# First-norm operands of a streaming encoder layer: conditioning products between the transposes, group 0 first, group 1 in place

## The chip, the cores and the metric

One Trainium2 chip, one of its cores. The metric is the device time of one execution in microseconds, taken as the median of several runs; the smaller the better. TensorE (PE) multiplies matrices, VectorE (DVE) and ScalarE (ACT) do elementwise work, GpSimd (POOL) too, and SyncE (SP) issues the DMA transfers. Each engine executes its own queue in order; semaphores hold one for another.

## The reference

One inference step of a hybrid encoder layer, for a prompt of 1024 tokens and a sample of 32 (1056 together), model width 1024. All arithmetic is float32:

```python
mod = (silu(c) @ w_ada + b_ada)               # shift1, scale1, gate1, shift2, scale2, gate2
h = rms_norm(x, norm1_g) * (1 + scale1) + shift1
proj = h @ w_in                               # 8192 columns: q, k, v, xin, gb, gc, ga, gb_br
...                                           # differential attention, short convolution, gates, output
x = x + gate1 * (m @ w_out)
h2 = rms_norm(x, norm2_g) * (1 + scale2) + shift2
x = x + gate2 * ((silu(g) * up) @ w_down)     # g, up = split(h2 @ w_gate_up)
```

The change concerns the first two lines only: how h comes to the form in which the first projections use it.

## The kernel before, in words

**Layout.** h is kept transposed in `xnT`: 128 partitions (a channel of one of 8 channel tiles) by 1056 tokens. The tokens are cut into four quarters of 264 columns (`QW`); quarters 0 and 2 are token group 0, quarters 1 and 3 are group 1.

**The multiplications.** `strassen` (from L164) multiplies a 256-column block of weights with one token group by a seven-product scheme in the order of `SEQ`: products on the operands B11, T2, T1, B21, T3, B22, T4, each of twelve matmuls (four channel tiles, three parts, because each float32 factor is split into a rounded high part and a remainder). B11, B12 are the two quarters of the group in channel tiles 0 to 3, B21, B22 those in tiles 4 to 7; T1 = B12 - B11, T2 = B22 - T1, T3 = B22 - B12, T4 = B21 - T2. The results are gathered in PSUM banks X, Y, Z, V: VectorE adds u2 = Y + p1 after product 2 (L188) and w = Z + u2 after product 3 (L191). Product 6 adds into Z again and product 7 into V, so product 6 waits until L191 has read Z and product 7 until L197 has read V.

**The operands.** `split` (L83 to L85) writes an operand: ScalarE casts the high part, VectorE subtracts it to get the remainder. `h_operands(j, g)` (from L389) does this for one channel tile pair j, j + 4 and one group g: four subtractions on VectorE (L398, L399, L403, L406) into small tiles `ht`, and seven splits, all of 264 columns. It is called eight times.

**The order around it.** Conditioning products come first: `ada_load` fetches a 1024 x 128 block of w_ada (seven buffers, shared with the weights), `ada_matmul` (L333) multiplies it, ScalarE copies the row (L335), `ada_close` transposes four rows (L342) and adds the bias (L344, `mod`). x is loaded in nine token tiles (L294), squared on ScalarE (L301), scaled on VectorE (L304), transposed on TensorE (L313) and copied to `xnT` (L315 on ScalarE, L317 on VectorE). `modulate(n)` takes its gain from L377 and applies gain and shift to the prompt's tokens on ScalarE (L384) and to the sample's on VectorE (L386), in place. The loop over j = 0 to 3 does four conditioning products, modulates tiles j and j + 4, and builds the operands of group 0 for j and of group 1 for j - 1; at j = 2 the first weights are split in between (`wstrassen`, L147 to L157, its last remainder on GpSimd). Then h is stored to DRAM (L445), the last group 1 operands follow, and `attention_constants` loads five small rows (L264) and takes an Exp (L271). The first projection `conv_in` runs group 0 and then group 1 with the same weights.

TensorE's queue is in the order of the program. On the other engines a scheduler orders the instructions when the program is built, by its own costs, so the place of an instruction in a queue is not that of its line.

Of the kernel before, what the change touches and what calls it, by code (L numbers as in the profile page):

```python
# [7 lines left out]
F32 = mybir.dt.float32  # L8
# [6 lines left out]
P = 128  # L15
D = 1024
KT = 8
S = 1024
DS = 32
T = S + DS  # L20
# [9 lines left out]
QW = T // 4  # L30
# [4 lines left out]
def f(ap):  # L35
    return ap.bitcast(F32)


def hybrid_layer(tc, x_prompt, x_sample, cache_k, cache_v, state_conv, c_prompt, c_sample,
# [76 lines left out]
    def u_tile():  # L116
        return PSB.tile([P, 512], F32, tag="u", name="u", bufs=6)

    def x_tile():
        return PSB.tile([P, 512], F32, tag="x", name="x", bufs=2)  # L120
# [7 lines left out]
    Top, home = {}, {}  # L128

    def op_slot(i, shape, dtype, name):  # L130
        return (OpA if i < NA else OpB).tile(shape, dtype, tag=f"op{i}", name=name)
# [4 lines left out]
    def wstrassen(srcs):  # L136

        raw = [kt_stage(src) for src in srcs]
        A11, A12, A21, A22 = raw[0][:, :4], raw[0][:, 4:], raw[1][:, :4], raw[1][:, 4:]
        w = {}  # L140

        def parts(o, src, eng=None):
            w[o] = ws_tile()
            split(src, w[o][:, 0], w[o][:, 1], eng)

        parts("A11", A11)
        dve.tensor_sub(A11, A11, A21)  # L147
        S3 = A11
        dve.tensor_add(A21, A21, A22)
        S1 = A21  # L150
        parts("A22", A22)
        dve.tensor_sub(A22, A22, S3)
        S2 = A22
        parts("S2", S2)
        parts("S1", S1)
        parts("A12", A12)
        dve.tensor_sub(A12, A12, S2)  # L157
        S4 = A12
        parts("S3", S3)
        parts("S4", S4, pool)  # L160
        return w
# [72 lines left out]
    E = sb("E", side="right")  # L234
    X0 = sb("X0")
# [6 lines left out]
    def load_rows():  # L242
        for r0, ap in ((R_B, b_ada), (R_G1, norm1_g), (R_G2, norm2_g), (R_CW, conv_w[0]), (R_ST, state_conv[0, 0])):
            row_load(rows[r0:r0 + ap.shape[0] * ap.shape[1] // P, :], ap)
        for u in range(2):
            sp.dma_start(rows[R_GQ:R_GQ + 1, u * HD:(u + 1) * HD], q_norm_g)
        sp.dma_start(rows[R_GS:R_GS + 1, :], sub_norm_g)

    def rows_to_vec():
        pv = x_tile()  # L250
        pe.transpose(pv[:, :P], rows, ident)
        dve.tensor_copy(vec, pv[:, :P])
# [24 lines left out]
    xnT = X0.tile([P, KT, T], F32, name="xnT")  # L277
# [3 lines left out]
    def token_tile(i):  # L281
        return (xp_v[i * P:(i + 1) * P, :], P) if i < 8 else (xs_v, DS)
# [3 lines left out]
    def x_half(i):  # L286
        if i // 2 not in xslots:
            xslots[i // 2] = op_slot(NA + i // 2, [P, 2, T], F32, "xt")
        return xslots[i // 2][:, i % 2, :D]

    def x_load(i):
        src, n = token_tile(i)
        xt = x_half(i)
        sp.dma_start(xt[:n], src)  # L294
        xts[i] = xt, n

    def x_norm(i):

        xt, n = xts[i]
        junk = x_half(9 + i % 2)  # L300
        act.activation(junk[:n], xt[:n], AF.Square, scale=1.0 / 32.0, accum_out=msx[:n, i:i + 1])  # L301
        pool.tensor_scalar(out=rsx[:n, i:i + 1], in0=msx[:n, i:i + 1], scalar1=EPS, scalar2=None, op0=ALU.add)
        pool.tensor_tensor(out=rsx[:n, i:i + 1], in0=rsx[:n, i:i + 1], in1=mhalf[:n, 0:1], op=ALU.pow)
        dve.tensor_scalar(out=xt[:n], in0=xt[:n], scalar1=rsx[:n, i:i + 1], scalar2=None, op0=ALU.mult)  # L304

    def x_transpose(tiles, kts):
        q0 = tiles[0] * P
        w = sum(xts[i][1] for i in tiles)
        for kt in kts:
            pt = u_tile()  # L310
            for j, i in enumerate(tiles):
                xt, n = xts[i]
                pe.transpose(pt[:, j * P:j * P + n], xt[:n, kt * P:(kt + 1) * P], ident[:n, :n])  # L313
            if kt % 2:
                act.copy(xnT[:, kt, q0:q0 + w], pt[:, :w])  # L315
            else:
                dve.tensor_copy(xnT[:, kt, q0:q0 + w], pt[:, :w])  # L317
# [3 lines left out]
    def ada_load(c):  # L321
        v = w_slot([P, KT, P], F32, "adw")
        sp.dma_start(v, wada_v[:, :, c * P:(c + 1) * P])
        ada_v.append((c, v))
# [3 lines left out]
    def ada_matmul():  # L328

        c, v = ada_v.pop(0)  # L330
        pa = x_tile()
        for kt in range(KT):
            pe.matmul(pa[0:2, :P], sc[:, kt:kt + 9:8], v[:, kt, :], start=kt == 0, stop=kt == KT - 1)  # L333
        row = E.tile([2, P], F32, tag=("w", "t")[len(ada_open) % 2], name="adarow", bufs=2)
        act.copy(row, pa[0:2, :P])  # L335
        ada_open.append((c, row))

    def ada_close():
        pb = x_tile()
        done, ada_open[:] = ada_open[:], []  # L340
        for i, (c, row) in enumerate(done):
            pe.transpose(pb[:, 2 * i:2 * i + 2], row, ident[0:2, 0:2])  # L342
        for i, (c, row) in enumerate(done):
            dve.tensor_scalar(out=mod[:, c, :], in0=pb[:, 2 * i:2 * i + 2], scalar1=vec[:, R_B + c:R_B + c + 1],  # L344
                              scalar2=None, op0=ALU.add)
# [30 lines left out]
    def scale_gain(dst, sec, n, row):  # L376
        dve.tensor_scalar(out=dst[:, n, :], in0=mod[:, sec * KT + n, :], scalar1=1.0,  # L377
                          scalar2=vec[:, row + n:row + n + 1], op0=ALU.add, op1=ALU.mult)

    def modulate(n):  # L380

        scale_gain(a1, 1, n, R_G1)
        y = xnT[:, n, 0:S]
        act.activation(y, y, AF.Identity, scale=a1[:, n, 0:1], bias=mod[:, n, 0:1])  # L384
        y = xnT[:, n, S:T]
        dve.tensor_scalar(out=y, in0=y, scalar1=a1[:, n, 1:2], scalar2=mod[:, n, 1:2], op0=ALU.mult, op1=ALU.add)  # L386

    def h_operands(j, g):

        def parts(o, src):  # L390
            t = Top[o, g]
            split(src, t[:, 0, j, :], t[:, 1, j, :])

        b11, b12 = (xnT[:, j, q * QW:(q + 1) * QW] for q in (g, g + 2))
        b21, b22 = (xnT[:, j + 4, q * QW:(q + 1) * QW] for q in (g, g + 2))
        t1, t2, t3 = (X0.tile([P, QW], F32, tag=f"t{i}", name="ht", bufs=1) for i in (1, 2, 1))
        parts("B11", b11)
        dve.tensor_sub(t1, b12, b11)  # L398
        dve.tensor_sub(t2, b22, t1)  # L399
        parts("T2", t2)  # L400
        parts("T1", t1)
        parts("B21", b21)
        dve.tensor_sub(t3, b22, b12)  # L403
        parts("T3", t3)
        parts("B22", b22)
        dve.tensor_sub(t2, b21, t2)  # L406
        parts("T4", t2)

    ada_order = [sec * KT + n for j in range(4) for n in (j, j + 4) for sec in (0, 1)]
    for c in ada_order[:4]:  # L410
        ada_load(c)
    load_rows()
    for i in range(9):
        x_load(i)
    for c in ada_order[4:7]:
        ada_load(c)
    for c in ada_order[7:11]:
        ada_matmul()
        ada_load(c)
    rows_to_vec()  # L420
    ada_close()
    for i in range(9):
        x_norm(i)
        if i % 4 == 3:
            x_transpose(range(i - 3, i + 1), range(KT))
    x_transpose((8,), range(KT))
    for i, (o, g) in enumerate((o, g) for o in OPS for g in (0, 1)):
        home[o, g] = (OpA if i < NA else OpB, f"op{i}")
        Top[o, g] = op_slot(i, [P, 2, 4, QW], F32R, f"{o}{g}")
    for j in range(4):  # L430
        if j:
            for i in range(4):
                ada_matmul()
                if 7 + 4 * j + i < len(ada_order):
                    ada_load(ada_order[7 + 4 * j + i])
            ada_close()
        if j == 2:
            w0 = wstrassen(win_pair(3, 0))
        modulate(j)
        modulate(j + 4)  # L440
        h_operands(j, 0)
        if j:
            h_operands(j - 1, 1)
    for n in range(KT):
        sp.dma_start(h_d[n], xnT[:, n, :])  # L445
    h_operands(3, 1)
    attention_constants()


# [93 lines left out]
    for sec, dst in ((6, ga_d), (7, gb_d)):  # L543
        for p in range(0, KT, 2):
            w = wstrassen(win_pair(sec, p))
            sg = pair_tile()
# [571 lines left out]
    for n in range(KT):  # L1118
        w = wpiece(wao_v[:, :, n * P:(n + 1) * P])
        sg = B.tile([P, T], F32, tag="sg", name="sg", bufs=2)  # L1120
# [5 lines left out]
        for g0, gw in GROUPS:  # L1126
            pt = u_tile()
            unit(pt, w, ot, g0, gw)
            c = slice(g0, g0 + gw)
# [203 lines left out]
    E = sb("E")  # L1333
# [92 lines left out]
    late = [slot(("T4", 0)), xk[:, 0], xk[:, 1]]  # L1426
# [102 lines left out]
```

## Time and profile before

| | us |
|---|---|
| median of 3 runs (2134.64 to 2137.19) | 2136.35 |
| the profiled execution: its own time | 2132.99 |
| its span, from first to last instruction | 2131.2 |
| TensorE busy / VectorE busy / ScalarE busy | 2031.0 / 1351.4 / 847.1 |
| mean granted TensorE clock, of full speed | 0.982 |

The profile page gives busy times per engine and the span in 40 slices; views of the trace give the stages, the instructions in order of time, and what each engine waited for. Times in the trace start at the span's first instruction. A bracket such as [0.93 <-DVE sg L197] says that the engine was idle for 0.93 us in front of the row and that L197 on VectorE ended it. Instructions overlap on an engine's pipeline, so the time from one start to the next can be shorter than the duration shown.

### The profile page before, as it was taken

The page shows a single profiled execution, that of the slowest core. Times are in us where ns is not written, and L with a number is a line of the kernel's source. Part 1 is how long each engine was busy: PE and PEld are TensorE (multiplying, and loading weights), DVE is VectorE, ACT ScalarE, POOL GpSimd, SP SyncE. Part 2 cuts the span into 40 slices and gives each one's busy share as a digit, 9 for nine tenths or more (in the row PEclk, how much of TensorE's full clock was granted, in tenths as well). Part 3 has the DMA queues.
Part 4 walks back from the last instruction along what each step waited for, and adds up shares of the span by engine and source line. Part 5 has one row for each costly group of instructions (what it writes and reads, how often), then busy time and mean ns, then how long its engine had stood idle before and what let it go on. Part 6 is the DMA issues. An engine that isn't in the chain of part 4 may idle for free. (4 is left out here: it accounts for less than half of the span.)

```text
span 2131.2 us, 37806 instructions
## 1 busy us (share of the span) xinstructions
PE 2031.0 (95%) x14339; PEld 1976.7 (93%) x14339; DVE 1351.4 (63%) x3096; ACT 847.1 (40%) x2044; POOL 364.7 (17%) x660
## 2 busy tenths in 40 slices
PE   7799999899999999999899989889999999999999
PEld 5799999899999999999899989879999999989998
DVE  4988799967766776677357974685555555432322
ACT  5522233366666666666222213463332332321210
POOL 1023100033333333333000000012112112100000
PEclk8899999999999999999999999999999999999999
DMA  8422254532211221121388625123222222552321
GB/s 251 151 84 90 71 161 135 192 89 60 68 57 56 62 59 54 50 69 48 114 258 250 198 90 170 53 68 122 71 73 89 70 80 79 172 157 65 99 69 57
DMA packets 298960, 224.42 MB, mean 105 GB/s; under 512 B 15617, under 2 KB 281498, under 8 KB 298778
## 3 DMA queue, kind: packets, MB, share of 16 engines
q1 hardware_dynamic: 298778, 222.00, 34.0%
q8 instruction: 113, 1.85, 0.4%
q14 instruction: 69, 0.57, 0.1%
HBM read 162.46 MB, written 59.49 MB: 104 GB/s over the span
## 5 line engine op out<-in xcount | busy, mean ns | idle before, releaser
L84 ACT CAST ws<-st 128x512 fp32r<-128x512 f32 x360 | 217.2, 615 | 564.4 <-PE u L181 172.9
L181 PE MATMUL u<-op,ws 128*128 128x264 f32 x3168 | 397.3, 285 | 7.8 <-ACT op L84 6.5
L181 PEld LDWEIGHTS u<-op,ws 128*128 128x128 f32 x3168 | 392.4, 189 | 8.4 <-ACT op L84 6.7
L85 DVE TENSOR_TENSOR ws<-st,ws 128x512 fp32r<-128x512 f32 (+1 forms) x322 | 222.6, 699 | 195.3 <-ACT ws L84 192.9
L181 PE MATMUL u<-T,ws 128*128 128x264 f32 x1536 | 198.5, 287 | 1.2 <-DVE sg L197 1.2
L181 PEld LDWEIGHTS u<-T,ws 128*128 128x128 f32 x1536 | 193.5, 190 | 1.8 <-DVE sg L197 1.8
L731 PE MATMUL b<-qw,hA 128*128 128x384 f32 x512 | 186.8, 365 | 2.5 <-DVE adred L366 1.2
L732 PE MATMUL b<-qw,hA 128*128 128x384 f32 x512 | 174.2, 340 | 0.6 <-DVE qw L688 0.6
L733 PE MATMUL b<-qw,hA 128*128 128x384 f32 x512 | 173.8, 339 | 0.0
L1431 PE MATMUL u<-ka,ws 128*128 128x352 f32 x480 | 156.8, 327 | 4.6 <-ACT ka L84 2.8
L1432 PE MATMUL u<-ka,ws 128*128 128x352 f32 x480 | 155.6, 324 | 2.3 <-DVE ka L85 2.3
L181 PE MATMUL u<-B,ws 128*128 128x264 f32 x1152 | 152.1, 287 | 4.6 <-ACT B L84 4.6
L1433 PE MATMUL u<-ka,ws 128*128 128x352 f32 x480 | 155.7, 324 | 0.0
L181 PEld LDWEIGHTS u<-B,ws 128*128 128x128 f32 x1152 | 145.6, 190 | 5.3 <-ACT B L84 4.9
L357 DVE SCALAR_TENSOR_TENSOR adacc<-adw,sc,adacc 128x128 f32<-128x128 f32 x448 | 132.8, 350 | 0.6
L879 ACT ACTIVATE p<-S,nmx,rs 128x128 f32<-128x128 f32 (+5 forms) x144 | 113.1, 787 | 50.1 <-DVE nmx L959 17.0
L85 POOL TENSOR_TENSOR ws<-st,ws 128x512 fp32r<-128x512 f32 x38 | 49.8, 1311 | 445.3 <-ACT ws L84 426.1
L731 PEld LDWEIGHTS b<-qw,hA 128*128 128x128 f32 x512 | 97.7, 191 | 6.4 <-issue 2.1
L732 PEld LDWEIGHTS b<-qw,hA 128*128 128x128 f32 x512 | 97.9, 191 | 1.2 <-DVE qw L688 0.9
L733 PEld LDWEIGHTS b<-qw,hA 128*128 128x128 f32 x512 | 97.2, 190 | 0.0
L1431 PEld LDWEIGHTS u<-ka,ws 128*128 128x128 f32 x480 | 90.6, 189 | 5.6 <-ACT ka L84 3.5
L1432 PEld LDWEIGHTS u<-ka,ws 128*128 128x128 f32 x480 | 90.7, 189 | 3.1 <-DVE ka L85 3.1
(277 smaller groups left out, 4379.8 us busy)
## 6 DMA issues: line engine op xcount, KB each, us to landing
adw<-in_w_ada_dram SPq DMA_DIRECT2D x48, 512.0 KB, 4.0
st<-in_w_gate_up_dram SPq DMA_DIRECT2D x44, 512.0 KB, 4.0
st<-in_w_in_dram SPq DMA_DIRECT2D x43, 512.0 KB, 4.3
sa<-a_d SPq DMA_DIRECT2D x22, 528.0 KB, 3.6
a_d<-xa SPq DMA_DIRECT2D x84, 132.0 KB, 1.7
st<-in_w_in_dram SPq DMA_DIRECT2D x42, 256.0 KB, 2.9
st<-in_w_down_dram SPq DMA_DIRECT2D x16, 512.0 KB, 5.0
h_d<-xnT SPq DMA_DIRECT2D x8, 528.0 KB, 4.3
```

Of the source, the lines that this page charges most:

```text
L84: act.copy(hi, src)
L85: (lo_eng or dve).tensor_sub(lo, src, f(hi))
L181: pe.matmul(q[dst], l, t[:, r, j, :], start=first and j == n == 0, stop=j == 3 and n == 2, skip_group_check=not first)
L357: dve.scalar_tensor_tensor(out=acc[:, s_, :], in0=st[:, kt, :], scalar=sc[:, 8 * s_ + kt:8 * s_ + kt + 1], in1=acc[:, s_, :], op0=ALU.mult ...
L731: pe.matmul(pj[:, 0:384], a, qh[:, :, c, :], start=kt == 0, stop=False)
L732: pe.matmul(pj[:, 0:384], a, ql[:, :, c, :], start=False, stop=False)
L733: pe.matmul(pj[:, 0:384], b, qh[:, :, c, :], start=False, stop=kt == KT - 1)
L879: act.activation(p[:n, :u["L"]], u["sv"][m][:n], AF.Exp, bias=u["nmx"][:n, m:m + 1], scale=u["rs_t"][:n, m:m + 1], accum_out=sums[:n, m:m ...
L1431: pe.matmul(pt[:, :gw], wh, ah, start=kt == 0, stop=False)
L1432: pe.matmul(pt[:, :gw], wh, al, start=False, stop=False)
L1433: pe.matmul(pt[:, :gw], wl, ah, start=False, stop=kt == KC - 1)
```

## The change

The call of `x_transpose` is cut in halves, and two conditioning products (`ada_two`) stand between the halves of a set of tiles; two of the w_ada loads go ahead of the x tiles 4 to 8. The operands of group 0 are built first: for j = 0 and 1 in one call on 528 columns, then for j = 2 and 3 on 264 each, in a new buffer `hs`. The first weights are split after the operands of j = 2. All operands of group 1 are built at the end by `h_operands_rest`, on 4 x 264 columns each, with the four subtractions written in place into `xnT`, in the order of use: which is possible only after the stores of h have read it.

```diff
-    def h_operands(j, g):
+    hs = E.tile([P, 2, T], F32, tag="sg", name="hs", bufs=1)
+
+    def h_operands(j, k):
...
-        b11, b12 = (xnT[:, j, q * QW:(q + 1) * QW] for q in (g, g + 2))
-        b21, b22 = (xnT[:, j + 4, q * QW:(q + 1) * QW] for q in (g, g + 2))
-        t1, t2, t3 = (X0.tile([P, QW], F32, tag=f"t{i}", name="ht", bufs=1) for i in (1, 2, 1))
+        b11, b12 = (xnT[:, j:k, q * QW:(q + 1) * QW] for q in (0, 2))
+        b21, b22 = (xnT[:, j + 4:k + 4, q * QW:(q + 1) * QW] for q in (0, 2))
+        t1, t2, t3 = (hs[:, i, :(k - j) * QW].rearrange("p (a b) -> p a b", b=QW) for i in (0, 1, 0))
...
+    def h_operands_rest():
...
+        b11, b12, b21, b22 = (xnT[:, 4 * i:4 * i + 4, q * QW:(q + 1) * QW] for i in (0, 1) for q in (1, 3))
+        parts("B11", b11)
+        dve.tensor_sub(b11, b12, b11)
+        parts("T1", b11)
+        dve.tensor_sub(b11, b22, b11)
+        parts("T2", b11)
+        parts("B21", b21)
+        dve.tensor_sub(b12, b22, b12)
+        parts("T3", b12)
+        parts("B22", b22)
+        dve.tensor_sub(b21, b21, b11)
+        parts("T4", b21)
...
-    for i in range(9):
+    for i in range(4):
         x_load(i)
-    for c in ada_order[4:7]:
+    for c in ada_order[4:6]:
         ada_load(c)
-    for c in ada_order[7:11]:
-        ada_matmul()
-        ada_load(c)
+    for i in range(4, 9):
+        x_load(i)
+    ada_load(ada_order[6])
...
-    for i in range(9):
+    for i in range(4):
         x_norm(i)
-        if i % 4 == 3:
-            x_transpose(range(i - 3, i + 1), range(KT))
+    x_transpose(range(0, 4), range(0, 4))
+    ada_two()
+    x_transpose(range(0, 4), range(4, KT))
+    for i in range(4, 9):
+        x_norm(i)
+    x_transpose(range(4, 8), range(0, 4))
+    ada_two()
+    x_transpose(range(4, 8), range(4, KT))
+    ada_close()
     x_transpose((8,), range(KT))
...
     for j in range(4):
+        if j > 1:
+            ada_two()
+            ada_two()
+            ada_close()
+        modulate(j)
+        modulate(j + 4)
         if j:
-            for i in range(4):
-                ada_matmul()
-                if 7 + 4 * j + i < len(ada_order):
-                    ada_load(ada_order[7 + 4 * j + i])
-            ada_close()
+            h_operands(0 if j == 1 else j, j + 1)
         if j == 2:
             w0 = wstrassen(win_pair(3, 0))
-        modulate(j)
-        modulate(j + 4)
-        h_operands(j, 0)
-        if j:
-            h_operands(j - 1, 1)
     for n in range(KT):
         sp.dma_start(h_d[n], xnT[:, n, :])
-    h_operands(3, 1)
+    h_operands_rest()
     attention_constants()
```

What that does to the queues is shown at three places. First VectorE around L188 and L191 of group 0's first projection. In a name such as T40_389 the last digit ahead of the underscore is the group: T40 is operand T4 of group 0, T21 is T2 of group 1. Before:

```order
L85 TENSOR_TENSOR T40_389<-ht_719,T40_389 128x264
L85 TENSOR_TENSOR T11_382<-ht_739,T11_382 128x264
L399 TENSOR_TENSOR ht_740<-xnT_115,ht_739 128x264
L188 TENSOR_TENSOR u2_834<-u_821,p1_819 128x264
L403 TENSOR_TENSOR ht_741<-xnT_115 128x264
L85 TENSOR_TENSOR T21_380<-ht_740,T21_380 128x264
L191 TENSOR_TENSOR w_849<-u_836,u2_834 128x264
```

And of the change, from the last operand of group 0 on:

```order
L85 TENSOR_TENSOR T40_451<-hs_120,T40_451 128x264
L418 TENSOR_TENSOR xnT_115<-xnT_115 128x4x264
L85 TENSOR_TENSOR B211_446<-xnT_115,B211_446 128x1056
L423 TENSOR_TENSOR xnT_115<-xnT_115 128x4x264
L85 TENSOR_TENSOR T11_444<-xnT_115,T11_444 128x1056
L85 TENSOR_TENSOR B221_450<-xnT_115,B221_450 128x1056
L420 TENSOR_TENSOR xnT_115<-xnT_115 128x4x264
L85 TENSOR_TENSOR T31_448<-xnT_115,T31_448 128x1056
L426 TENSOR_TENSOR xnT_115<-xnT_115 128x4x264
L85 TENSOR_TENSOR T21_442<-xnT_115,T21_442 128x1056
L188 TENSOR_TENSOR u2_739<-u_726,p1_724 128x264
L85 TENSOR_TENSOR T41_452<-xnT_115,T41_452 128x1056
```

L191 is the row behind the last one. L188 and L191 stood between narrow instructions of group 1; now all wide ones of group 1 stand ahead of them.

Second, ScalarE around the last modulation (the L384 pair of tiles 3 and 7) and the Exp of the attention constants (L271). Before:

```order
L384 ACTIVATE xnT<-xnT,mod,a_118 128x1024 x2
L84 CAST B_377<-xnT 128x264
L84 CAST T_381<-ht 128x264
L84 CAST T_379<-ht 128x264
L84 CAST B_383<-xnT 128x264
L84 CAST B_387<-xnT 128x264
L84 CAST B_378<-xnT 128x264
L84 CAST B_384<-xnT 128x264
L84 CAST B_388<-xnT 128x264
L84 CAST T_385<-ht 128x264
L271 ACT_TABLE_LOAD
L271 ACTIVATE lsum<-lsum 128x2
```

And of the change:

```order
L335 COPY adarow<-x 2x128
L271 ACT_TABLE_LOAD
L271 ACTIVATE lsum<-lsum 128x2
L84 CAST ws<-st 128x512
L335 COPY adarow<-x 2x128
L384 ACTIVATE xnT<-xnT,mod,a_118 128x1024 x2
L84 CAST B_439<-xnT 128x264
```

The Exp has moved from behind the last modulation to a place ahead of it, and the copy of the last conditioning row (the second L335) stands behind the Exp.

Third, SyncE's issues of the stores of h (`h_d`), the constants (`gk`, `lams`) and the second weights (`st`). Before:

```order
L445 DMA h_d<-xnT 128x1056 x4
L264 DMA gk<-in_k_norm_g_dram 128x64
L264 DMA lams<-in_lambda_q_dram 128x64 x2
L445 DMA h_d<-xnT 128x1056
L264 DMA lams<-in_lambda_k_dram 128x64 x2
L445 DMA h_d<-xnT 128x1056
L107 DMA st<-in_w_in_dram 128x8x128 x2
L445 DMA h_d<-xnT 128x1056 x2
```

And of the change:

```order
L479 DMA h_d<-xnT 128x1056 x6
L264 DMA gk<-in_k_norm_g_dram 128x64
L264 DMA lams<-in_lambda_q_dram 128x64 x2
L264 DMA lams<-in_lambda_k_dram 128x64 x2
L107 DMA st<-in_w_in_dram 128x8x128 x2
L479 DMA h_d<-xnT 128x1056 x2
```

The first two constants stood behind four stores, the rest behind a fifth; now all five stand behind six.

## Rows read from the trace of the kernel before

**Rows 1.** The page: the span, busy time of each engine with its share and number of instructions, and TensorE in 40 equal slices, in tenths.

```profile
span 2131.2 us, 37806 instructions
PE 2031.0 (95%) x14339; PEld 1976.7 (93%) x14339; DVE 1351.4 (63%) x3096; ACT 847.1 (40%) x2044; POOL 364.7 (17%) x660
PE   7799999899999999999899989889999999999999
```

**Rows 2.** Stages of the first 240 us: the stretch, its length, then busy us of each engine with the number of instructions, the granted TensorE clock, the DMA engines' share and GB/s.

```profile
core 0: us, PE busy (x) PEld busy (x) DVE busy (x) ACT busy (x) POOL busy (x), PEclk, DMA share, GB/s
46.00:57.00 11.00, 7.30 (x67) 5.32 (x64) 7.28 (x25) 7.46 (x19) 0.00 (x0) 1.00 1.04 305
57.00:70.29 13.29, 7.92 (x69) 5.85 (x70) 13.11 (x32) 9.54 (x22) 1.38 (x1) 0.95 0.55 207
70.29:77.27 6.98, 2.35 (x10) 2.04 (x9) 6.94 (x26) 5.15 (x11) 0.00 (x0) 0.50 0.55 163
77.27:86.09 8.82, 8.82 (x50) 8.52 (x51) 7.96 (x25) 6.72 (x18) 0.00 (x0) 0.69 0.24 94
86.09:99.40 13.31, 13.31 (x111) 13.31 (x110) 11.68 (x29) 5.43 (x11) 0.44 (x4) 1.00 0.29 80
99.40:240.00 140.60, 139.67 (x1141) 139.46 (x1140) 114.44 (x229) 35.41 (x68) 36.10 (x56) 1.00 0.27 84
```

**Rows 3.** TensorE's instructions in order of time, from the conditioning products on: start, us from the first start to the last end of the merged instructions, line, operation, tiles and shape, count, and the idle time ahead with what ended it.

```profile
38.02 7.15 PE L333 MATMUL x<-adw,sc 128*2 128x128 f32 x64
...
70.29 2.35 PE L181 MATMUL u<-B,ws 128*128 128x264 f32 x9
77.27 1.39 PE L181 MATMUL u<-B,ws 128*128 128x264 f32 x3 [4.63 <-ACT B L84]
78.46 5.00 PE L181 MATMUL u<-T,ws 128*128 128x264 f32 x24
83.30 1.61 PE L181 MATMUL u<-B,ws 128*128 128x264 f32 x12
84.75 1.64 PE L181 MATMUL u<-T,ws 128*128 128x264 f32 x12
86.22 1.64 PE L181 MATMUL u<-B,ws 128*128 128x264 f32 x12
87.70 1.62 PE L181 MATMUL u<-T,ws 128*128 128x264 f32 x12
89.15 1.64 PE L181 MATMUL u<-B,ws 128*128 128x264 f32 x12
90.63 3.09 PE L181 MATMUL u<-T,ws 128*128 128x264 f32 x24
...
99.44 1.76 PE L181 MATMUL u<-B,ws 128*128 128x264 f32 x13
```

**Rows 4.** VectorE up to 92 us, grouped by line and shape: count, then busy us and mean ns of one, then idle time ahead.

```profile
L85 DVE TENSOR_TENSOR T<-ht,T 128x264 fp32r<-128x264 f32 x32 | 13.0, 426 | 2.3 <-ACT T L84 2.3
L85 DVE TENSOR_TENSOR B<-xnT,B 128x264 fp32r<-128x264 f32 x24 | 9.9, 428 | 0.3 <-ACT B L84 0.3
...
L399 DVE TENSOR_TENSOR ht<-xnT,ht 128x264 f32<-128x264 f32 x8 | 3.4, 427 | 0.7 <-ACT xnT L384 0.7
```

**Rows 5.** VectorE in order of time around L188 and L191.

```profile
82.44 0.42 DVE L399 TENSOR_TENSOR ht<-xnT,ht 128x264 f32<-128x264 f32 x1
82.79 0.42 DVE L188 TENSOR_TENSOR u<-u,p 128x264 f32<-128x264 f32 x1
83.13 0.42 DVE L403 TENSOR_TENSOR ht<-xnT 128x264 f32<-128x264 f32 x1
83.47 0.43 DVE L85 TENSOR_TENSOR T<-ht,T 128x264 fp32r<-128x264 f32 x1
83.81 0.43 DVE L191 TENSOR_TENSOR w<-u,u 128x264 f32<-128x264 f32 x1
```

**Rows 6.** ScalarE in order of time: weight casts, the last modulations and the Exp.

```profile
62.94 2.16 ACT L84 CAST ws<-st 128x512 fp32r<-128x512 f32 x4
...
74.55 2.37 ACT L384 ACTIVATE xnT<-xnT,mod,a 128x1024 f32<-128x1024 f32 x2
...
79.80 1.28 ACT L271 ACT_TABLE_LOAD   x1
81.09 0.20 ACT L271 ACTIVATE lsum<-lsum 128x2 f32<-128x2 f32 x1
```

**Rows 7.** VectorE in order of time in a later stage, with instructions of 1056 columns.

```profile
1371.19 1.25 DVE L1261 TENSOR_TENSOR h<-h,h 128x1056 f32<-128x1056 f32 x1
1372.36 1.25 DVE L1258 TENSOR_TENSOR h<-h,h 128x1056 f32<-128x1056 f32 x1
```

**Rows 8.** SyncE's issues in order of time; then, for the tiles of the constants and of the stores, the issue's duration in ns (least, median, most) and the time from issue to landing.

```profile
56.33 1.18 SPq L264 DMA_DIRECT2D gk<-in_k_norm_g_dram  x1
57.56 2.33 SPq L264 DMA_DIRECT2D lams<-in_lambda_q_dram  x2
...
63.43 2.07 SPq L264 DMA_DIRECT2D lams<-in_lambda_k_dram  x2
...
66.70 2.54 SPq L107 DMA_DIRECT2D st<-in_w_in_dram  x2
...
L264 SPq DMA_DIRECT2D lams<-in_lambda_k_dram x2: 445/1011/1577, 63.4 to 65.1; - x2
DMA to landing us min/median/max: 4.4/5.0/5.6
...
DMA to landing us min/median/max: 2.7/4.3/5.9
```

**Rows 9.** GpSimd's weight remainder, and VectorE's subtraction at the same time.

```profile
67.46 1.38 POOL L85 TENSOR_TENSOR ws<-st,ws 128x512 fp32r<-128x512 f32 x1 [34.62 <-ACT ws L84]
...
67.74 1.38 DVE L403 TENSOR_TENSOR ht<-xnT 128x264 f32<-128x264 f32 x1
```

**Rows 10.** What TensorE waited for from 99 to 260 us: us in total, times, longest.

```profile
PE u L181 <- DVE sg L197: 0.9, 1, 0.9
```

More of the change, by code (lines that the diff above doesn't have):

```diff
@@ L386, in modulate @@
         dve.tensor_scalar(out=y, in0=y, scalar1=a1[:, n, 1:2], scalar2=mod[:, n, 1:2], op0=ALU.mult, op1=ALU.add)
-    def h_operands(j, g):
+    hs = E.tile([P, 2, T], F32, tag="sg", name="hs", bufs=1)
+    def h_operands(j, k):
         def parts(o, src):
-            t = Top[o, g]
-            split(src, t[:, 0, j, :], t[:, 1, j, :])
-        b11, b12 = (xnT[:, j, q * QW:(q + 1) * QW] for q in (g, g + 2))
-        b21, b22 = (xnT[:, j + 4, q * QW:(q + 1) * QW] for q in (g, g + 2))
-        t1, t2, t3 = (X0.tile([P, QW], F32, tag=f"t{i}", name="ht", bufs=1) for i in (1, 2, 1))
+            t = Top[o, 0]
+            split(src, t[:, 0, j:k, :], t[:, 1, j:k, :])
+        b11, b12 = (xnT[:, j:k, q * QW:(q + 1) * QW] for q in (0, 2))
+        b21, b22 = (xnT[:, j + 4:k + 4, q * QW:(q + 1) * QW] for q in (0, 2))
+        t1, t2, t3 = (hs[:, i, :(k - j) * QW].rearrange("p (a b) -> p a b", b=QW) for i in (0, 1, 0))
         parts("B11", b11)
@@ L407, in h_operands, with parts @@
         parts("T4", t2)
+    def h_operands_rest():
+        def parts(o, src):
+            split(src, Top[o, 1][:, 0], Top[o, 1][:, 1])
+        b11, b12, b21, b22 = (xnT[:, 4 * i:4 * i + 4, q * QW:(q + 1) * QW] for i in (0, 1) for q in (1, 3))
[10 more added lines that the diff above has]
+        parts("T4", b21)
     ada_order = [sec * KT + n for j in range(4) for n in (j, j + 4) for sec in (0, 1)]
@@ L412, in hybrid_layer, with ada_two @@
     load_rows()
-    for i in range(9):
+    for i in range(4):
         x_load(i)
-    for c in ada_order[4:7]:
+    for c in ada_order[4:6]:
         ada_load(c)
-    for c in ada_order[7:11]:
-        ada_matmul()
-        ada_load(c)
+    for i in range(4, 9):
+        x_load(i)
+    ada_load(ada_order[6])
+    late = list(ada_order[7:])
+    def ada_two():
+        for _ in range(2):
+            ada_matmul()
+            if late:
+                ada_load(late.pop(0))
+    ada_two()
+    ada_two()
     rows_to_vec()
     ada_close()
-    for i in range(9):
+    for i in range(4):
         x_norm(i)
-        if i % 4 == 3:
-            x_transpose(range(i - 3, i + 1), range(KT))
+    x_transpose(range(0, 4), range(0, 4))
[7 more added lines that the diff above has]
+    ada_close()
     x_transpose((8,), range(KT))
@@ L430, in hybrid_layer @@
     for j in range(4):
-        if j:
-            for i in range(4):
-                ada_matmul()
-                if 7 + 4 * j + i < len(ada_order):
-                    ada_load(ada_order[7 + 4 * j + i])
-            ada_close()
+        if j > 1:
+            ada_two()
+            ada_two()
+            ada_close()
+        modulate(j)
+        modulate(j + 4)
+        if j:
+            h_operands(0 if j == 1 else j, j + 1)
         if j == 2:
             w0 = wstrassen(win_pair(3, 0))
-        modulate(j)
-        modulate(j + 4)
-        h_operands(j, 0)
-        if j:
-            h_operands(j - 1, 1)
     for n in range(KT):
         sp.dma_start(h_d[n], xnT[:, n, :])
-    h_operands(3, 1)
+    h_operands_rest()
     attention_constants()
```

## The prediction

> **What bounds the kernel now.** The page comes first: TensorE is busy for 2031.0 of 2131.2 us, and of its 40 slices the first two alone fall to 7 and 7 [rows 1]. The change touches only what lies in these two slices, so the next view is the stages of the first 240 us [rows 2]. From 99.4 us on TensorE idles 0.93 of 140.6 us: behind that point the kernel is TensorE's own queue, and the end moves by as much as that point moves. Ahead of it TensorE is the one that waits: from 70.29 to 77.27 us it works 2.35 of 6.98 us, while VectorE works 6.94 of them, and 13.11 of the 13.29 us before.
>
> TensorE's own rows [rows 3] name the pieces. At 70.29 it starts product 1 of the first projection (operand B11 of token group 0), does nine of its twelve matmuls, and idles 4.63 us for the last quarter of B11, the one of j=3. [...] Products 6 and 7 of group 0 start at 86.22 and 87.70, group 1 at 89.15, the next weights at 99.44: nine products, 13.2 us, without idle time.
>
> Who is late ahead of that: each call of the old helper is four subtractions and seven remainders of 264 columns, 427 ns each [rows 4], 0.345 us from start to start (82.44, 82.79, 83.13 [rows 5]). Eight calls are 88 of them, 30.4 us. Three calls for group 1 stand in front of the last modulation, which ScalarE starts at 74.55 [rows 6].
>
> Operands are not all that TensorE needs. Product 6 adds into the PSUM bank Z, which L191 must have read; L191 needs L188. Now these two run on VectorE at 82.79 and 83.81 [rows 5], between group 1's subtractions, and product 6 follows product 5 without a gap [rows 3]. That is what I look for in the new order.
>
> **The change, part by part.**
>
> *The last modulation.* The three group 1 calls in front of it go: 33 x 0.345 = 11.4 us of VectorE. Two narrow group 0 calls become one of 528 columns, estimated at 0.62 us from start to start, between 0.345 for 264 and 1.17 for 1056 (1371.19 to 1372.36 [rows 7]); this saves 11 x (0.69 - 0.62) = 0.8. If VectorE alone set the moment, it would be 74.55 - 12.2 = 62.3. It does not any more: on ScalarE the new order puts the last modulation behind the fourth conditioning row, and that row behind the Exp of the attention constants, which used to come after the modulation, at 81.09 [rows 6]. Exp waits for VectorE's product of the lambda rows, and that for five small transfers (gk and four lambda rows), whose issue takes SyncE 1.18 + 2.33 + 2.07 = 5.6 us [rows 8] and whose landing takes 4.4 to 5.6 us from the issue [rows 8]. They now follow the stores of h for j=2. That j is modulated at about 58.8: the transposes and eight conditioning products that TensorE had done at 45.7 (38.02 + 7.15 and the small transposes [rows 3]) are the same ones in another order, two modulated pairs follow (2 x 2.37), then eleven instructions of 0.62, two of weights, and the row of conditioning. So the stores leave at about 61.2, the last constant is issued near 66 and lands near 70.5. Product, reduction, Exp, the last weight cast, the row's copy and transpose, and the modulation values are some 2.5 to 3.5 us: **73**. Ends: 69 if the constants are issued at 0.45 us each, as the second lambda_k was (2.07 less 1.58 for the first), and 75 if they queue behind the stores for longer and GpSimd's weight remainder stalls VectorE, which in the old run stretched a 427 ns subtraction to 1.38 us beside GpSimd's 1.38 [rows 9]. I take 73, since the issue times were long in four of five cases.
>
> *From there to product 6.* VectorE's new order is the heart of this prediction: L188 stands behind ten wide instructions of group 1, L191 behind an eleventh. From the second subtraction (it needs both modulations, 73 + 2.37 = 75.4) I count ten narrow ones, 10 x 0.345 = 3.5; eleven of 1056 columns (four in-place subtractions and seven remainders) at 1.17, 12.9; L188 and L191, 0.7; waits between dependent neighbours, 0.2. Sum 17.3: L191 is done at **92.7**, and with it product 6 starts, where it started at 86.22. That is +6.5 us. TensorE can do products 1 to 5 from about 76.5 and is through by 85: it then stands for some 7 us. The in-place subtractions also wait for the stores of h, of which the last two are issued after the last modulation; such stores took 2.7 us to land at the least [rows 8]. L418 comes at about 80, so these are hidden by VectorE's own 5 us of narrow work; if that cover fails, rival 3 holds.
>
> *Behind product 6.* The same nine products follow, 13.2 us at full clock. After such a gap the clock was 0.50 last time [rows 2], and 24 matmuls took 5.00 instead of 3.09 us [rows 3]: +1.9. Bounds 0 and 2; I take 2, for the gap is longer than the 4.63 us that went before the slow rows. So the next weights start at 92.7 + 13.2 + 1.9 = 107.8 instead of 99.44.
>
> *The rest.* Two conditioning loads of 512 KB now go ahead of x tiles 4 to 8 and delay them by some 3.5 us (at the 305 GB/s of 46 to 57 us [rows 2]); the conditioning products stand between the transposes and use that time on TensorE, and the transfers run without the pause that the late products made. All of that ends ahead of 58.8 and is in it. ScalarE's casts (four of 512 columns in 2.16 us [rows 6]) stay under VectorE's 0.62 each. Past the first projection pair the engines' orders are the same as before, and TensorE's queue is shifted as a whole; only its one later wait, 0.9 us on L197 [rows 10], should go, since VectorE then leads: -0.9.
>
> Sum: 6.5 + 1.9 - 0.9 = **+7.5 us**, on the profiled execution's 2132.99 us (span 2131.2) 2140.5. The median of the runs, 2136.35, stands 3.4 above that execution; so 2143.9.
>
> [...]
>
> **The rivals.**
>
> 1. *The relief arrives: faster.* If the constants land early enough and VectorE alone sets the last modulation, it comes at 62.3, L191 at 62.3 + 2.4 + 17.3 = 82.0, and product 6 starts at 82 instead of 86.22: 2136.35 - 4.2 = 2132. [...] It decides below 66.5, where L191 comes no later than 86.2. Against it: the conditioning rows and the constants cannot be in by then, by the sum above.
> 2. *About no change.* The constants' transfers do not hold Exp, the last modulation is at 69, the clock stays up: 6.5 - 4 + 0 - 0.9, +1.6; with half of that, +3.3: 2138 to 2140.
> 3. *Slower still.* The stores of the last two h tiles are issued behind the two weight loads that stand ahead of them on SyncE and wait for GpSimd; L418 then waits in VectorE's queue with L191 behind it. Loads of 512 KB took 2.54 us for two to be issued [rows 8], so 3 to 4 us more: 2147 to 2148.
>
> **How the numbers follow.** Forecast 0.62, rival 1 0.07, rival 2 0.18, rival 3 0.13. The range runs from the low bound, 2143.9 - 4 - 2 = 2138, to 2143.9 + 2 + 3 = 2149. A measurement can tell about 0.2%, 4.3 us. Slower by more than that is the forecast and rival 3, 0.75; within it rival 2, 0.18; faster 0.07.
>
> **What would show it.** In the new profile: an idle stretch of TensorE of 5 to 9 us in front of a product on B22 of group 0, ended by VectorE L191; L188 at about 90, ahead of T4's wide remainder; the Exp ahead of the last modulation, that one near 73; wide VectorE rows of about 1.25 us end to end with no idle time. If TensorE instead runs from product 1 through 14 without a gap, or the last modulation comes before 66, the prediction is wrong.

## The result, and the profile of the changed kernel

Six runs of the changed kernel gave a median of 2144.57 us (2138.15 to 2146.36) against 2135.02 us for six of the kernel before: ratio 1.0039, 95% interval 1.0029 to 1.0049. Twelve runs of a later measurement gave 2142.92 against 2137.53, 1.0023 (1.0012 to 1.0033). The change makes the kernel slower, by 9.6 us between the first two medians and 5.4 between the second two. (A ratio is estimated from all runs of a measurement and need not be the quotient of the two medians.) The profiled execution of the changed kernel is the fastest of the six (2138.15 us, span 2136.4).

The page of the changed kernel, the lines that answer to [rows 1]:

```profile
span 2136.4 us, 37736 instructions
PE 2033.6 (95%) x14339; PEld 1976.7 (93%) x14339; DVE 1348.4 (63%) x3052; ACT 843.8 (39%) x2016; POOL 366.3 (17%) x660
PE   6799999899999999999899989889999999999998
```

VectorE has 44 instructions less and 3.0 us less work, TensorE the same 14339 matmuls. Nothing on the page names a loss of 5 us; of the 40 slices of TensorE only the first (6 instead of 7) and the last (8 instead of 9) differ.

TensorE in order of time, answering to [rows 3] (start, us to the last end, line, tiles, count, and in brackets the idle time ahead with what ended it):

```profile
62.79 5.32 PE L333 MATMUL x<-adw,sc 128*2 128x128 f32 x32 [3.54 <-ACT adarow L335]
...
69.12 1.36 PE L181 MATMUL u<-B,ws 128*128 128x264 f32 x9
72.92 1.02 PE L181 MATMUL u<-B,ws 128*128 128x264 f32 x3 [2.43 <-ACT B L84]
73.77 4.61 PE L181 MATMUL u<-T,ws 128*128 128x264 f32 x24
78.23 1.61 PE L181 MATMUL u<-B,ws 128*128 128x264 f32 x12
79.67 1.63 PE L181 MATMUL u<-T,ws 128*128 128x264 f32 x12
89.72 3.01 PE L181 MATMUL u<-B,ws 128*128 128x264 f32 x12 [8.41 <-DVE w L191]
92.52 2.59 PE L181 MATMUL u<-T,ws 128*128 128x264 f32 x12
94.95 1.62 PE L181 MATMUL u<-B,ws 128*128 128x264 f32 x12
...
105.22 3.10 PE L181 MATMUL u<-B,ws 128*128 128x264 f32 x24
```

Products 1 to 5 are over earlier than before (the fifth ends at 81.3 instead of 86.4), then TensorE stands for 8.41 us in front of product 6, and the releaser is L191. Products 6 and 7 take 5.23 us (89.72 to 94.95) instead of 2.93 at [rows 3]: the clock has fallen, to a mean of 0.53 granted over that stretch (the row below). The next weights start at 105.22 instead of 99.44. In three pieces, against [rows 3]: product 1 comes 1.17 us earlier, from product 1 to product 6 it takes 20.60 instead of 15.93 (+4.67), from there to the next weights 15.50 instead of 13.22 (+2.28); the sum is +5.78. The stretch of products 6 and 7 (length, busy us of TensorE and count, granted clock, DMA share, GB/s):

```profile
89.70:95.00 5.30, 5.28 (x25) 0.53 0.73 198
```

VectorE, answering to [rows 5, 7]:

```profile
71.46 0.43 DVE L400 TENSOR_TENSOR hs<-xnT 128x264 f32<-128x264 f32 x1 [0.76 <-ACT xnT L384]
72.59 0.43 DVE L401 TENSOR_TENSOR hs<-xnT,hs 128x264 f32<-128x264 f32 x1 [0.70 <-ACT xnT L384]
...
75.35 1.25 DVE L85 TENSOR_TENSOR B<-xnT,B 128x1056 fp32r<-128x1056 f32 x1
76.52 0.77 DVE L85 TENSOR_TENSOR T<-hs,T 128x264 fp32r<-128x264 f32 x2
77.21 1.25 DVE L418 TENSOR_TENSOR xnT<-xnT 128x1056 f32<-128x1056 f32 x1
78.38 1.25 DVE L85 TENSOR_TENSOR B<-xnT,B 128x1056 fp32r<-128x1056 f32 x1
...
87.73 0.42 DVE L188 TENSOR_TENSOR u<-u,p 128x264 f32<-128x264 f32 x1
88.07 1.25 DVE L85 TENSOR_TENSOR T<-xnT,T 128x1056 fp32r<-128x1056 f32 x1
89.24 0.42 DVE L191 TENSOR_TENSOR w<-u,u 128x264 f32<-128x264 f32 x1
```

Ten wide instructions stand ahead of L188, one more between it and L191, 1.17 us from start to start. Nothing waits: busy time of that stretch, from L401 to L191's end (length, then busy us and count, clock, DMA share, GB/s), is the stretch itself:

```profile
72.59:89.66 17.07, 17.07 (x23) 0.75 0.22 82
```

ScalarE and SyncE, answering to [rows 6, 8]:

```profile
66.11 1.28 ACT L271 ACT_TABLE_LOAD   x1
67.60 0.20 ACT L271 ACTIVATE lsum<-lsum 128x2 f32<-128x2 f32 x1 [0.20 <-DVE lsum L270]
...
70.19 2.37 ACT L384 ACTIVATE xnT<-xnT,mod,a 128x1024 f32<-128x1024 f32 x2 [1.27 <-DVE a L377]
```

```profile
59.24 0.45 SPq L264 DMA_DIRECT2D gk<-in_k_norm_g_dram  x1
59.73 1.43 SPq L264 DMA_DIRECT2D lams<-in_lambda_q_dram  x2
61.20 0.91 SPq L264 DMA_DIRECT2D lams<-in_lambda_k_dram  x2
```

The Exp is ahead of the last modulation, as the order said, but the constants were issued in 2.8 us, not 5.6, and the modulation came at 70.19. (In the order before, three of the five constants stood behind four stores, gk and two rows of lambda, and two behind a fifth.)

### The profile page after: what moved, and what is told of

Its sections match the earlier page's. It is cut to its first block, busy times and chain, and to the rows that moved or that the text cites. A ratio compares the mean times of both kernels' runs of the same rounds, so it can differ in the third digit from the quotient of the medians.

```text
span 2136.4 us, 37736 instructions
## 1 busy us (share of the span) xinstructions
PE 2033.6 (95%) x14339; PEld 1976.7 (93%) x14339; DVE 1348.4 (63%) x3052; ACT 843.8 (39%) x2016; POOL 366.3 (17%) x660
```

## The experiments

Theory A: the second group's operand code, queued on VectorE ahead of L188 and L191, holds product 6, and the clock falls in the gap. Rival B: the second group's operands would be late in any place. Rival C: the new head costs the time. A side question is the constants, on which the prediction put the moment of the last modulation. In the table, the places of the products are those of the one profiled execution of each kernel. The ratio is to runs of the kernel before that were made alongside: their median was 2135.02 for changed; 2136.22 for the two halves, rest_behind_group0 and constants_late; 2137.53 for changed_again, rest_narrow, rest_and_constants_late and narrow_rest_and_constants_late; and 2136.13 for new_head_old_again, narrow_both_again and narrow_rest_late. So ratios may be compared across the rows, medians only within such a group.

| kernel | median us | ratio (95%) | product 1 | product 6 (idle ahead) | next weights | product 1 to next weights |
|---|---|---|---|---|---|---|
| before | 2136.35 | 1 | 70.29 | 86.22 (0) | 99.44 | 29.15 |
| changed | 2144.57 | 1.0039 (1.0029 to 1.0049) | 69.12 | 89.72 (8.41) | 105.22 | 36.10 |
| changed_again | 2142.92 | 1.0023 (1.0012 to 1.0033) | 69.28 | 89.87 (8.41) | 105.35 | 36.07 |
| old_head_new_operands | 2144.98 | 1.0050 (1.0036 to 1.0063) | 70.08 | 91.69 (7.57) | 107.66 | 37.58 |
| new_head_old_operands | 2133.91 | 0.9991 (0.9983 to 1.0000) | 69.05 | 84.69 (0) | 97.91 | 28.86 |
| new_head_old_again | 2136.25 | 0.9990 (0.9980 to 1.0001) | 71.05 | 86.56 (0) | 99.77 | 28.72 |
| rest_behind_group0 | 2137.17 | 1.0012 (1.0002 to 1.0022) | 69.44 | 81.47 (0) | 96.63 | 27.19 |
| constants_late | 2142.77 | 1.0033 (1.0020 to 1.0045) | 67.83 | 88.41 (8.53) | 103.38 | 35.55 |
| rest_narrow | 2140.91 | 1.0013 (1.0002 to 1.0025) | 69.09 | 88.53 (5.40) | 104.12 | 35.03 |
| rest_and_constants_late | 2137.91 | 1.0003 (0.9991 to 1.0016) | 69.31 | 81.35 (0) | 96.18 | 26.87 |
| narrow_rest_and_constants_late | 2133.88 | 0.9979 (0.9970 to 0.9988) | 69.33 | 83.14 (0) | 96.96 | 27.63 |
| narrow_both_again | 2133.86 | 0.9986 (0.9976 to 0.9996) | 69.12 | 81.82 (0) | 95.65 | 26.53 |
| narrow_rest_late | 2137.34 | 1.0005 (0.9996 to 1.0015) | 72.20 | 86.12 (0) | 100.56 | 28.36 |

The last column is the steadiest: two executions of one kernel differ there by 0.03, 0.14 and 1.1 us, while their ends differ by nearly 4.

### The two halves of the change, each alone

```diff
 # new_head_old_operands: the changed kernel with the operand code of before
...
-        if j:
-            h_operands(0 if j == 1 else j, j + 1)
         if j == 2:
             w0 = wstrassen(win_pair(3, 0))
+        h_operands(j, 0)
+        if j:
+            h_operands(j - 1, 1)
...
-    h_operands_rest()
+    h_operands(3, 1)
```

> The changed loading, modulation products and transposes, with the operand code of the kernel before (narrow, one of the 8 rows of tiles at a time, the second group one step behind the first, no sums in place). Theory A (only the order of the operand code costs): L188 and L191 stand as in the kernel before, product 6 waits as there (4.6 us of idle time around product 1, none at 6); 2135 (2132 to 2138). Rival C (the modulation products between the transposes cost the time, through the operands or the loads of weights): 2140 to 2146.

```diff
 # old_head_new_operands: the kernel before with the changed operand code
...
-        h_operands(j, 0)
-        if j:
-            h_operands(j - 1, 1)
+        if j:
+            h_operands(0 if j == 1 else j, j + 1)
...
-    h_operands(3, 1)
+    h_operands_rest()
```

> The head of the kernel before (all transposes, then the modulation products step by step), with the changed operand code: first group's sums through the loop, second group's in place, in wide instructions, behind all of them. Theory A: product 6 waits for L191 behind nine wide instructions as in the changed kernel, 8 to 9 us of idle time; 2145 (2142 to 2148). Rival C (the head is what costs): 2133 to 2138.

In both, the first weights are split ahead of the operands of j = 2, as in the kernel before; that small part of the change is in neither half.

Measured: 2133.91 and 2144.98. The head alone costs nothing and may give 2 us (the interval ends at 1.0000; a repeat below reads 0.9990, up to 1.0001); the operand code alone is the whole loss. Rival C falls. TensorE with the old head and the new code, then with the new head and the old code:

```profile
82.51 1.62 PE L181 MATMUL u<-T,ws 128*128 128x264 f32 x12
91.69 3.01 PE L181 MATMUL u<-B,ws 128*128 128x264 f32 x12 [7.57 <-DVE w L191]
```

```profile
75.42 1.32 PE L181 MATMUL u<-B,ws 128*128 128x264 f32 x3 [4.02 <-ACT B L84]
...
83.22 1.64 PE L181 MATMUL u<-T,ws 128*128 128x264 f32 x12
84.69 1.64 PE L181 MATMUL u<-B,ws 128*128 128x264 f32 x12
```

In the second, product 6 follows product 5 as it did before, and the idle time sits in product 1 again [rows 3].

### The same wide instructions, behind L188 and L191

```diff
-    h_operands_rest()
     attention_constants()
...
             conv_in(w0, p, (0,), xin)
+            h_operands_rest()
             w = w0
```

> The second group's operand code is called behind the first group's products, with nothing else changed; in VectorE's queue L188 then stands ahead of all wide instructions and L191 behind one of them instead of nine. Theory A (the queue holds product 6): product 6 follows product 5 without the 8.4 us of idle time at TensorE, at about 81.5 instead of 89.7; the second group's T2 is then the late one, ready about 85 to 87, for some 2 us of idle time there; the next weights at 93 to 96 instead of 105.2. About 10 us below the changed kernel's 2144.6: 2134.5 (2131 to 2138). Rival B (the second group's wide products are late wherever they stand in the queue, so the idle time only moves from product 6 to the second group's products 2 and 5): 2141 to 2145. Rival C (the new head costs the time): 2142 or more.

Measured: 2137.17, 1.0012. TensorE:

```profile
81.47 1.62 PE L181 MATMUL u<-B,ws 128*128 128x264 f32 x12
...
87.83 3.10 PE L181 MATMUL u<-T,ws 128*128 128x264 f32 x23 [1.17 <-DVE T L85]
...
96.63 3.11 PE L181 MATMUL u<-B,ws 128*128 128x264 f32 x24
...
139.34 4.47 PE L181 MATMUL u<-T,ws 128*128 128x264 f32 x24 [2.98 <-DVE sg L197]
```

The 8.41 us are gone, with no instruction less; the second group waits 1.2 us for its T2. That is theory A, and rival B falls. The next weights come at 96.63, 8.6 us earlier than in the changed kernel; the expectation had 93 to 96 and a time of 2134.5, and the measured gain is 7.4 us of the first median (5.8 of the second). Of the 8.6 us, more than 4 are given back at 139: TensorE waits 2.98 us for L197 in the next pair of columns, the clock falls behind the gap (0.67 granted from 139.34 to 143.65), and the 24 matmuls take 4.47 us, where the same product of the changed kernel starts at 144.97, waits 0.47 and takes 3.19. That leaves some 4.4 us, which is less than the medians show; the difference is not traced. Ahead of that L197 VectorE had idled 1.49 us for the next weights' transfer and done five pieces of the later conditioning (some 1.4 us), which the changed kernel does not have at that place; that these two make up the wait is worked out and not tested. From 125 to 150 us (busy us and count, clock, DMA share, GB/s), here and in the changed kernel:

```profile
125.00:150.00 25.00, 21.15 (x159) 0.93 0.50 149
```

```profile
125.00:150.00 25.00, 24.39 (x194) 1.00 0.33 107
```

### The constants

```diff
-    attention_constants()
...
             conv_in(w0, p, (0,), xin)
+            attention_constants()
```

> The attention constants (four lams loads, Exp with its table load, their VectorE instructions) are set up behind the first group's products instead of ahead; all else as in the changed kernel. Theory A (they no longer hold the last modulation, since the lams landed at 65.5 and Exp was done at 67.8, ahead of the last adarow): last modulation 0.5 to 1 us earlier than 70.2, product 6 still idle for some 8 us, time 2143.5 (2141.5 to 2145). Rival (the constants ahead of the last modulation cost what the prediction put on them, 3 to 4 us): 2140 to 2141.

Measured: 2142.77, inside the range of theory A; not told apart from the changed kernel's two medians. Its trace has product 1 at 67.83, 1.3 us earlier, and it would be easy to credit the constants alone. The rows name two causes. One is that the last 32 conditioning matmuls took 3.66 us instead of the 5.32 above:

```profile
63.16 3.66 PE L333 MATMUL x<-adw,sc 128*2 128x128 f32 x32 [3.54 <-ACT adarow L335]
```

From 63.00 to 66.70 us TensorE's granted clock (after busy us and count) was 0.63 in the changed kernel and 1.00 here:

```profile
63.00:66.70 3.70, 3.70 (x24) 0.63 0.19 45
```

```profile
63.00:66.70 3.70, 3.54 (x32) 1.00 0.04 10
```

The idle time ahead is the same 3.54 us in both. The other cause is the Exp, which is no longer in the way. With the constants in front, the Exp and those matmuls end almost together, and ScalarE's next cast and the last row's copy stand behind both. The changed kernel, done with the Exp at 67.80, still waits for TensorE (first row); in its second execution, changed_again, the Exp itself waits for the lambda sums, and the cast follows it without a wait for TensorE (second and third row):

```profile
68.15 0.62 ACT L84 CAST ws<-st 128x512 fp32r<-128x512 f32 x1 [0.35 <-PE x L333]
```

```profile
68.21 0.20 ACT L271 ACTIVATE lsum<-lsum 128x2 f32<-128x2 f32 x1 [0.91 <-DVE lsum L270]
68.32 0.60 ACT L84 CAST ws<-st 128x512 fp32r<-128x512 f32 x1
```

In rest_behind_group0 the Exp is the last too. From the start of the 32 matmuls to product 1 it takes 6.33 us where TensorE is the last (changed, and rest_and_constants_late, which has the constants moved and the 5.32 us again), and 6.52 and 6.57 where the Exp is (changed_again, rest_behind_group0). So at the fallen clock the constants cost 0.2 us or nothing; a full clock alone could have given the changed kernel's first execution no more than those 0.35 us; the 1.3 us came where both were away. The times of the runs are too coarse to show any of this.

### Narrow instead of wide, in the same place

```diff
     def h_operands_rest():
...
-        b11, b12, b21, b22 = (xnT[:, 4 * i:4 * i + 4, q * QW:(q + 1) * QW] for i in (0, 1) for q in (1, 3))
+        for j in range(4):
+            b11, b12, b21, b22 = (xnT[:, 4 * i + j, q * QW:(q + 1) * QW] for i in (0, 1) for q in (1, 3))
...
```

> The second group's sums stay in place and stay where the change calls them, but in instructions of 264 columns, one row of tiles at a time, instead of 4 x 264. Those of the first three rows of tiles do not need the last modulation, so the scheduler puts them into VectorE's queue ahead of it; between L401 and L191 then stand some 36 narrow instructions instead of 10 narrow and 11 wide. Theory A (what counts is VectorE's work queued between the last modulation and L191): 36 x 0.343 = 12.3 us instead of 17.1, so product 6 is some 4.7 us earlier, at about 85; some 4 us of idle time left; 2140 (2137.5 to 2142). Rival (four narrow instructions take 1.37 us where a wide one takes 1.17, and group 0's own operands are delayed by them): 2144 to 2147.

Measured: 2140.91, in theory A's range. The first three rows' sums got ahead of the last modulation and less work stands between L401 and L191, as expected, but product 6 came at 88.53, not 85: L401 started at 73.35, not 72.59, and up to L191's end VectorE took 15.1 us. The longest wait in that stretch was for ScalarE's cast, which stood behind a copy out of PSUM (L501) for which ScalarE had waited 2.72 us for TensorE:

```profile
82.47 0.43 DVE L85 TENSOR_TENSOR T<-xnT,T 128x264 fp32r<-128x264 f32 x1 [2.17 <-ACT T L84]
```

```profile
88.53 3.01 PE L181 MATMUL u<-B,ws 128*128 128x264 f32 x12 [5.40 <-DVE w L191]
```

The direction is theory A's, the size was not: I had counted VectorE's work and not the other engine's.

### Both moved, wide and narrow

```diff
-    h_operands_rest()
-    attention_constants()
...
             conv_in(w0, p, (0,), xin)
+            h_operands_rest()
+            attention_constants()
```

The second kernel has this and the loop of rest_narrow; narrow_rest_late, further down, has the loop and moves `h_operands_rest()` alone.

> Both calls, the second group's operand code (wide, in place) and the attention constants, stand behind the first group's products. Theory A: what each did alone adds up: 2137.2 for the operand code moved, less 1.8 for the constants moved: 2135.4 (2132.5 to 2138); product 1 at about 68, no wait at product 6, next weights at about 95. Rival (Exp, its table load and the lams now stand in the way of the second group's copies): next weights at 97 or later, 2137 to 2140.

> As rest_and_constants_late, with the second group's instructions narrow (264 columns, one row of tiles at a time, in place). The first rows' sums can then run ahead of the last modulation, while L188 and L191 stand only some 10 narrow instructions behind L401. Theory A (each of the two causes gone: no queue ahead of L191, no wide T2 that comes late): product 6 right behind product 5, no idle time above 1 us in the second group, next weights at 92 to 95; 2132 (2129.5 to 2135), at or below new_head_old_operands. Rival (the time comes back in the next pair of columns, where VectorE's modulation pieces now collide with L197 as in rest_behind_group0, 3 us of idle time at TensorE and a half-clock stretch): 2135 to 2138.

Measured: 2137.91 and 2133.88. The wide one lies at the upper end of its range, in the rival's too, as the constants gave nothing. The narrow one's time is in its range, but its next weights, at 96.96, are not (92 to 95), and the wait for L197 that its rival named is there, 2.23 us at 137.53. It lies below the kernel before and the changed one, and is the version to keep, together with new_head_old_operands, from which its interval does not part it. Four more runs, three of them of unaltered kernels, show how far that can be trusted:

> The changed kernel once more, unaltered, on the chip of the other runs of this call. Its first profiled execution (2138.2) lay 6 us below its other five (2143.7 to 2146.4), and stood only 4.4 us behind the profiled execution of before at the end, 5.8 behind it where the first conv stage ends. Theory A1 (the size in the head is as in the first trace, and executions differ by some us of half-clock stretches in later stages): the trace again has product 6 at 89 to 90.5 and the first conv stage's end 5 to 7 us behind, and the remainder sits later; median 2143 to 2145.5. Rival (most executions lose more in the head than the first trace showed): the stage's end 9 us or more behind.

> narrow_rest_and_constants_late once more, unaltered. Theory A: median 2132 to 2136, below the kernel before and the changed one; in the trace product 6 follows product 5, next weights at about 97, and the wait for L197 near 138 (2.2 us with a half-clock stretch behind it) is there again. Rival (the first measurement, 4 us below a kernel that its trace hardly tells apart, was chance): within 1.5 us of the kernel before.

> new_head_old_operands once more, unaltered, on the same chip. Theory A: again some 2 us below the kernel before (1 to 4), next weights at about 98 against 99.4 of before; this says whether the second group's code made narrow and moved adds anything to what the head gives alone. Rival: no difference from the kernel before (within 1 us).

> As narrow_rest_and_constants_late, with the attention constants where the changed kernel has them, so that only the second group's operand code is moved and made narrow. Theory A (the constants cost next to nothing: between rest_behind_group0 and rest_and_constants_late the next weights moved by 0.45 us, and the 1.9 us of constants_late were one half-clock stretch that its profiled execution did not have): within 2 us of narrow_rest_and_constants_late, 2132 to 2137. Rival (the lams wait and Exp ahead of the last modulation cost their 2 us or more): 2136 to 2139 and the first product of the first group 1.5 us or more later than there (69.3).

The changed kernel's head is the same to 0.2 us in the second execution (product 6 at 89.87, idle time 8.41), while the two ends lie 3.9 us apart: at the first convolution stage's end, near 420, they are 5.75 and 5.59 us behind the kernel before, and at TensorE's last instruction 4.41 and 8.35. The loss of the change in the head is the 5.6 to 5.8; the 3.9 us at the end lie between two executions of one and the same kernel.

The new head with the old operand code again has 0.9990, but its interval takes in 1, and its median, 2136.25, is that of the kernel before alongside, 2136.13: a gain over before is not shown. The narrow version held (2133.86, 0.9986). Its wait behind the second weights is there again, now at 136.69, this time without a fallen clock (1.00 granted from 125 to 150 us; 0.93 in the first execution):

```profile
136.69 3.20 PE L181 MATMUL u<-T,ws 128*128 128x264 f32 x24 [2.29 <-DVE sg L197]
```

With the constants in front (narrow_rest_late) the median is 3.5 us higher, as the rival had it, though the two intervals touch at 0.9996. The trace doesn't show why: it is of the slowest of the eleven executions, which was already late at 38.82, long ahead of the constants, where its first 32 conditioning matmuls took 5.14 us and the repeat's 3.66:

```profile
38.82 5.14 PE L333 MATMUL x<-adw,sc 128*2 128x128 f32 x32
```

```profile
36.34 3.66 PE L333 MATMUL x<-adw,sc 128*2 128x128 f32 x32
```

From its last conditioning matmuls, at 65.95, to product 1 it took 6.25 us, and the repeat 6.33 (62.79 to 69.12): the constants did not hold product 1 there. Two things stay open: those 3.5 us, and why the narrow version's medians are 4 us below those of the wide one (rest_and_constants_late), when their traces have product 1 to the next weights within 0.8 us.

## Why the prediction was right, step by step

**The last modulation: wrong in size, half right in its reason.** Predicted 73, behind the constants; it came at 70.19. The stores ahead of the constants were issued by 59.2 and not 61.2, and gk and the lambda rows in 2.8 us, 0.45 us each but for one, so that the Exp was done at 67.80. In that execution the Exp was not even the last: TensorE's last 32 conditioning matmuls, which the prediction did not have as a limit, waited 3.54 us for a copied row, took 5.32 us at a fallen clock (0.63 granted from 63.00 to 66.70) and held ScalarE 0.35 us longer. In changed_again and rest_behind_group0 the Exp was the last, by some 0.2 us. The low end of 69 had the short issues as its reason, and these came; that a second limit ended so close to the first was chance.

**From there to product 6: right.** From the second subtraction to L191's end 17.3 us were summed and 17.07 measured, back to back, in the order that was read from the program. Starting 2.8 us earlier, it ended at 89.66 instead of 92.7, so product 6 was late by 3.50 and not 6.5. The idle time of 8.41, predicted as some 7, has the same releaser. L418 waited for no store: rival 3 did not come, its cover of narrow work held.

**The clock: right.** +1.9 predicted, +2.28 measured. Rival 2 had the modulation at 69, which was nearly so, and needed the clock to stay up, which it did not, at 0.53 over products 6 and 7 (its second number, +3.3, does not follow from its terms; half of the 4 us gives +3.6); rival 1 needed a modulation before 66.5.

**The later wait: half.** 0.9 us at [rows 10] was to go; 0.5 is left:

```profile
PE u L181 <- DVE sg L197: 0.5, 1, 0.5
```

**The sum.** +3.50 + 2.28 - 0.4 = +5.4 by the trace against the predicted +7.5. The second measurement is +5.4, the first +8.2 against the median that the sum was set on. The forecast's 2143.9 lies between the two medians; that it met the first within 1 us owes something to the modulation's being put 2.8 us too late, and the mechanism, not the size, is what the runs bear out.

**Wide instructions.** On VectorE they were the cheaper ones: from start to start four of 264 columns took 4 x 0.345 = 1.38 us [rows 5] and one of 1056 columns 1.17 (77.21 to 78.38 above), and VectorE's work fell by 3.0 us (1351.4 to 1348.4). But the 3.0 us bought nothing: in the same place the narrow, dearer instructions left 5.40 us of idle time instead of 8.41, since those of the first three rows of tiles ran ahead of the last modulation (in rest_narrow a subtraction of L424 at 69.24, the modulation at 70.86), for which a wide one has to wait (the first came at 75.35, the modulation at 70.19). The runs' times do not part the two for certain: 1.0013 (up to 1.0025) for the narrow ones, 1.0039 and 1.0023 (from 1.0012) for the wide.

## What to carry to other kernels

Before making an engine's instructions fewer and larger, look for what stands behind them in its queue: here an addition of 0.42 us (L191) that frees a PSUM bank for TensorE stood behind eleven instructions of 1.17 us each from start to start, and the 3 us saved cost 5 to 6 in the head. The cure is to put the short instruction that another engine waits for ahead of the bulk work, by calling the bulk code behind it. Here that alone took most of the loss away and no more (1.0012), since part of it came back at a later wait; below the kernel before came only the version with narrow instructions as well and the constants moved. And one trace's gain of 1 or 2 us is to be read row by row before it is credited to the edit, as a different clock in the same rows can make it (0.63 and 1.00 over the last conditioning products here), and two limits that end together can each hide what the other costs (here the Exp and those products, 0.2 and 0.35 us).

## What was not expected of the hardware

The same instructions behind the same idle time did not always get the same clock: after 3.54 us of idle time, 32 conditioning matmuls ran at a granted clock of 0.63 (from 63.00 to 66.70 us) in the changed kernel and of 1.00 in constants_late, 5.32 against 3.66 us, with the same instructions ahead of them on TensorE. Two executions of one kernel show it too: from 784 to 800 us, where TensorE idles 2.49 us for L982 in both, the changed kernel's granted clock was 1.00 and changed_again's 0.89, and 92 matmuls kept TensorE busy for 15.63 us there where 94 took 14.65 (busy us and count, clock, DMA share, GB/s):

```profile
784.00:800.00 16.00, 14.65 (x94) 1.00 0.31 88
```

```profile
784.00:800.00 16.00, 15.63 (x92) 0.89 0.31 88
```

After 8.41 us the products were slow both times (0.53 granted from 89.70 to 95.00 us in both). Two executions of one kernel ended nearly 4 us apart (spans of 2136.4 and 2140.2 for changed and changed_again, 2130.8 and 2134.5 for the two of the new head with the old operand code), which is more than some of the edits move; how much of that lies in stretches like these was not shown.
